# Three small changes of order in a hybrid attention block: where gate weights are prepared, where powers are taken, which weights are loaded first

## The chip, the cores and the metric

The kernel runs on one core of a Trainium2 chip, as one launch. The metric is device time in microseconds (us): the median of several runs of the kernel on the chip. Besides the runs there is one execution with the hardware profiler on. The core's engines are named as in the profile: TensorE is PE (with PEld for its weight loads), VectorE is DVE, ScalarE is ACT, GpSimd is POOL, SyncE is SP, and SPq is SP's queue, which issues nearly all transfers (DMA) of this kernel in one order.

## What is computed

A decoder layer of one sequence of 1024 tokens with 1024 features, in float32:

```
h    = rmsnorm(x)
proj = h @ w_in        # sliding-window q, k, v | query latents (384) | key/value latents (256)
                       # | rope key (32) | gate_a (1024) | gate_b (1024)
A    = sliding-window attention (8 heads, 2 key/value heads, window 128, a learned sink per head)
B    = latent attention: q = rmsnorm(q_lat) @ w_uq, k and v = rmsnorm(kv_lat) @ w_ukv, causal, 8 heads
y    = sigmoid(gate_a) * (A @ w_o_swa) + sigmoid(gate_b) * (B @ w_o_mla)
x    = x + y @ w_out
x    = x + (silu(h2 @ w_gate) * (h2 @ w_up)) @ w_down,   h2 = rmsnorm(x)
out  = rmsnorm(x)
```

## The kernel before

**Products.** Every float32 operand is split into a rounded high part and the rest, `hi` on ACT (line 159, a cast) and `lo` on DVE (line 162, a subtraction), and a product is three matmuls (lines 168 to 170). So each weight tile passes DMA, ACT and DVE before PE can use it. The large products are cut once into 2 x 2 blocks and done with seven block products in place of eight, named 1, 6, 2, 7, 5, 4, 3 in the order that they are taken. Sums of weight blocks that this needs are made on POOL (`mix`, `lower`). Products 1, 2, 5 and 3 add up in one PSUM bank (`fa`), products 6, 7 and 4 in another (`fb`). Between two of a bank's products its content is read out: after product 6 DVE adds `fb` and a saved tile into `pu` (`pu<-fb`), and only then may product 7 start to overwrite or add to `fb`.

**The gates.** The class `Seven` does the products for the 2048 gate columns, in eight groups j of seven products. `prep` splits the weights of one product (`wl`), `prep_to(n)` prepares up to the n-th product, `product` issues the next product's twelve matmuls on PE, and `copy_out` reads its bank. In `product` (line 685) the weights are prepared two products ahead, since `n_ahead` is 3. `gate_step` (line 746) runs one product with its read-out and then stores results that are ready.

**The stages.** The order of the first stage is written out by hand, as a string of two-letter steps (`ROWS`), and holds for all five engines. Its last rows begin the gates: `gp` is `prep_to`, `gx` is `product`, `ge` is `copy_out`; `gp5` stands behind `gx3 ge2 rr`. `rr` is a rotation of the rope key on POOL (`kr`, line 1051), and right behind the rows `kr` is stored. Then a loop of 15 iterations does the sliding-window attention, with three gate products in each as work for PE. One iteration has: transposes of the last block's probabilities (`pT<-per`, line 874), transposes of the queries, normalization of the present block's probabilities on POOL (`den` and `pe`, lines 844 to 847), the move of `pe` to `per` by DMA on SP's queue, the product with the values (`o`), and the next block's scores (`sc`), their maxima (line 816), shifts (`nm`, `es`) and exponentials (line 840).

The same loop also finishes the statistics of the latents: PE sums squares (line 765) into a spare piece of PSUM, `lat_stats` (line 1132) scales them on DVE into `rlat`, and, when both halves of the sequence are there, takes the power -1/2 of 8 columns on POOL (line 1137). That call stands ahead of the iteration's normalization, in iterations 2 (key/value latents) and 4 (query latents). `lat_tail` holds what follows at the end of an iteration: `lat_diag` in iteration 2 builds diagonals from the result on POOL (`dg`, line 1144), and `lat_norm` uses them on PE in iterations 3 and 5. The query part of `rlat` is first read in the latent attention.

**Behind the loop** five latent tiles (`ct`, line 1205) come back from DRAM, the two of keys and values first, then the three of queries; the weights for queries, keys and values (`uq`, `ukv`, lines 259 and 279) are loaded, split (`wuq`, `wv`) and used, `k<-ct,wv` for keys and `q<-ct,wuq` for queries, among the last four gate products. In the loop PE, SP and POOL keep the order of the program and a scheduler places ACT and DVE; behind the loop the scheduler, which works by its own estimate of times, places all of them.

Of the kernel before, what the change touches and what calls it, by code (L numbers as in the profile page):

```python
# [12 lines left out]
ALU = mybir.AluOpType  # L13
# [7 lines left out]
NB = S // P  # L21
# [66 lines left out]
def hybrid_block_kernel(  # L88
# [27 lines left out]
    nc = tc.nc  # L116
# [23 lines left out]
    def U(name, dt=F32, shape=(P, 1024)):  # L140
        return pool.tile(list(shape), dt, tag="u", name=uid(name))
# [7 lines left out]
    def P1(name, shape=(P, 512), dt=F32):  # L149
        return ps1.tile(list(shape), dt, tag="ps", name=uid(name))  # L150

    def PX(name, shape=(P, 512), dt=F32):
        return psum["x"].tile(list(shape), dt, tag="ps", name=uid(name))
# [3 lines left out]
    def split(hi, lo, src, eng=None):  # L157

        i = nc.scalar.copy(hi, src)  # L159
        if held[0]:  # L160
            tc.keep_in_program_order(i)
        (eng or nc.vector).tensor_tensor(lo, src, hi.bitcast(F32), op=ALU.subtract)  # L162

    def mm3(ps, pairs, first=True, last=True, go_on=False):

        n = len(pairs)
        for i, ((ah, al), (bh, bl)) in enumerate(pairs):
            nc.tensor.matmul(ps, ah, bh, start=first and i == 0, stop=False, skip_group_check=go_on)  # L168
            nc.tensor.matmul(ps, ah, bl, start=False, stop=False, skip_group_check=go_on)  # L169
            nc.tensor.matmul(ps, al, bh, start=False, stop=last and i == n - 1, skip_group_check=go_on)  # L170
# [10 lines left out]
    def half(s):  # L181
        return slice(512 * s, 512 * s + 512)
# [11 lines left out]
    rlat = const.tile([P, 2 * NB], F32, name="rlat")  # L194
    neg_half_w = const.tile([P, 2 * NB], F32, name="neg_half_w")
# [24 lines left out]
    st = Stream()  # L220
# [373 lines left out]
    class Seven:  # L594
# [87 lines left out]
            self.copy_out(*step)  # L682
            return step

        def product(self):
            j, q, m = self.seq[self.n_run]
            self.prep_to(self.n_run + self.n_ahead)
            self.n_run += 1
            if m == self.ms[0]:
                for what, *args in self.at.get((j, q), ()):  # L690
                    {"load": self.load_part, "mix": self.mix, "scale": self.scale_part}[what](*args)
            t = self.left.pop((j, q, m))
            if q in (1, 5):
                self.acc[("A", j, m)] = P1("fa")
            if q == 6:
                self.acc[("B", j, m)] = PX("fb")
            ps = self.acc[("A" if q in (1, 2, 5, 3) else "B", j, m)]
            rh, rl = hq[B_OF[q]]
            mm3(ps, [((t[:, 0, k], t[:, 1, k]), (rh[:, k], rl[:, k])) for k in range(4)], first=q in (1, 6, 5),
                go_on=q in (2, 7, 4, 3))  # L700
            return j, q, m
# [44 lines left out]
    def gate_step():  # L746
        late = gate_stores[:]
        gate_stores.clear()
        gates.run()
        for d, t in late:  # L750
            nc.sync.dma_start(d, t)

    gates = Seven(NK, "g", load_gate, gate_done, 3, (1, 6), 5, scale=scale_gate, scale_at=[(2, 0, 0, 2), (2, 0, 2, 2), (7, 1, 0, 2), (7, 1, 2, 2)], piece=2, vec=(2, 5))
# [347 lines left out]
    def small_tables():  # L1101
# [7 lines left out]
             "sl": load_set, "ss": set_sub, "sh": set_hi, "so": set_lo, "sf": set_four, "ph": phase, "tb": small_tables,  # L1109
             "ns": lambda: nc.vector.tensor_scalar(nsink, nsink, -1.0, None, op0=ALU.mult),  # L1110
             "gl": gates.load_part, "gs": gates.scale_part, "gm": gates.mix, "gp": gates.prep_to, "wq": sw_q, "wt": sw_qT,
             "gy": lambda j: gates.lower(j, "g"), "gx": lambda n: gates.product(),
             "ge": lambda n: gates.copy_out(*gates.seq[n - 1]), "wu": sw_q_hi, "wv": sw_q_lo,
             "wr": lambda it: sw_products(it, range(2)), "wm": lambda it: (sw_max(it, range(2)), sw_shift(it)),
             "we": sw_exp, "no": lambda it: sw[it].pop("norm")(), "mv": lambda it: nc.sync.dma_start(*sw[it].pop("move")),
# [11 lines left out]
    def lat_first():  # L1127
        ps = P1("st", (P, 4))
        sums(ps, 1, 0)
        lat_stats(ps, 1, 0)  # L1130

    def lat_stats(ps, grp, sh):
        c = slice(NB * grp + 4 * sh, NB * grp + 4 * sh + 4)
        nc.vector.tensor_scalar(rlat[:, c], ps[:, 0:4], -1.0 / (QL, KVL)[grp], EPS, op0=ALU.mult, op1=ALU.add)
        if sh:
            c = slice(NB * grp, NB * grp + NB)
            nc.gpsimd.tensor_tensor(rlat[:, c], rlat[:, c], neg_half_w[:, c], op=ALU.pow)

    def lat_diag():
        kvn["ones"] = U("ones", F32, (P, P))  # L1140
        nc.vector.memset(kvn["ones"], 1.0)
        kvn["dg"] = U("dg", F32, (P, NB, P))
        for b in range(NB):
            nc.gpsimd.tensor_scalar(kvn["dg"][:, b], ident, rlat[:, NB + b:NB + b + 1], 0.0, op0=ALU.mult, op1=ALU.add)

    def lat_norm(sh):
        ps = P1("rb", (P, 4, P))
        for b in range(4):
            nc.tensor.matmul(ps[:, b], kvn["ones"], kvn["dg"][:, 4 * sh + b], start=True, stop=True)
        for c in (3, 4):  # L1150
            y = klr[c][:, half(sh)]
            nc.vector.scalar_tensor_tensor(y, y, latg[:, c:c + 1], ps.rearrange("p b c -> p (b c)"), op0=ALU.mult,
                                           op1=ALU.mult)

    def kv_split(sh):
        for c in (3, 4):
            t = kvn[(c, sh)] = U("cs", F32R, (P, 2, 512))
            split(t[:, 0], t[:, 1], klr[c][:, half(sh)])

    def kv_store(sh):  # L1160
        for c in (3, 4):
            nc.sync.dma_start(ct_d[c][:, sh], kvn.pop((c, sh)).bitcast(F32))

    lat_tail = {1: lat_first, 2: lat_diag, 3: lambda: lat_norm(0), 4: lambda: kv_split(0),
                5: lambda: (kv_store(0), lat_norm(1)), 6: lambda: kv_split(1), 7: lambda: kv_store(1)}
    pool_order = tc.manual_schedule(engines={engines.Pool})
    pool_order.__enter__()
    for it in range(1, N_SW):
        if it + 2 < N_SW:
            sw_q(it + 2)  # L1170
        gate_step()
        sw_pT(it - 1)
        if it + 1 < N_SW:
            sw_qT_all(it + 1)
        if it in stats_at:
            lat_stats(spare[0], *stats_at[it])
        sw[it].pop("norm")()
        gate_step()
        nc.sync.dma_start(*sw[it].pop("move"))
        sw_pv(it - 1)  # L1180
        if it + 1 < N_SW:
            sw_scores(it + 1)
        gate_step()
        if it in lat_tail:
            lat_tail[it]()
# [16 lines left out]
    def load_ct(c):  # L1202
        t = V("ct", F32R, (P, 2, S))
        for sh in range(2):
            nc.sync.dma_start(t[:, :, half(sh)].bitcast(F32), ct_d[c][:, sh])
        lat_t.append((t[:, 0], t[:, 1]))
# [3 lines left out]
    for c in range(3, 5):  # L1210
        load_ct(c)
    gate_step()
    for c in range(3):
        load_ct(c)
    gate_step()
    st.load_to(st.index[("ukv", 1)])
    st.conv_to(st.index[("uq", 0)])
    gate_step()
    gate_step()
# [293 lines left out]
    for t in range(NT):  # L1513
        h, n = divmod(t, NB)
# [16 lines left out]
        if t in fill:  # L1531
            dc, sh, c0 = fill[t]
# [452 lines left out]
    while ffn.n_run < len(ffn.seq):  # L1985
        j, q, m = ffn.run()
# [211 lines left out]
```

## Time and profile before

| what | value |
|---|---|
| median of 3 runs | 1330.21 us (1328.77 to 1330.64) |
| the profiled execution: its time, its span | 1328.35 us, 1326.6 us |
| PE busy, share of the span | 1305.6 us, 98% |
| DVE, ACT, POOL busy | 928.5, 647.1, 587.7 us |
| gates' first products, sliding-window loop, weights and latents behind it | from about 136, 145 to 324, 320 to 345 us of the span |
| moved by DMA | 254.22 MB, mean 192 GB/s |

All times in rows are microseconds from the start of the span. A row of the timeline has its start, its length, the engine, the line, the operation, what is written and what is read (tile names without their numbers), and in brackets how long the engine stood idle before it and what ended that. A row of the waits has the waiting engine and line, what it waited for, and the total, the count and the longest wait in us. Matmuls are pipelined, so that a row's length is more than the distance from one start to the next; distances between starts are what counts for PE.

### The profile page before, as it was taken

The page shows a single profiled execution, that of the slowest core. Times are in us where ns is not written, and L with a number is a line of the kernel's source. Part 1 is how long each engine was busy: PE and PEld are TensorE (multiplying, and loading weights), DVE is VectorE, ACT ScalarE, POOL GpSimd, SP SyncE. Part 2 cuts the span into 40 slices and gives each one's busy share as a digit, 9 for nine tenths or more (in the row PEclk, how much of TensorE's full clock was granted, in tenths as well). Part 3 has the DMA queues.
Part 4 walks back from the last instruction along what each step waited for, and adds up shares of the span by engine and source line. Part 5 has one row for each costly group of instructions (what it writes and reads, how often), then busy time and mean ns, then how long its engine had stood idle before and what let it go on. Part 6 is the DMA issues. An engine that isn't in the chain of part 4 may idle for free.

```text
span 1326.6 us, 18712 instructions
## 1 busy us (share of the span) xinstructions
PE 1305.6 (98%) x6368; PEld 1093.4 (82%) x6368; DVE 928.5 (70%) x1451; ACT 647.1 (49%) x1285; POOL 587.7 (44%) x628
## 2 busy tenths in 40 slices
PE   9999899999999999999999999999999999999997
PEld 7987788888788889888888888888888888888886
DVE  7996678786577777887879756656676554663853
ACT  7586457666366666754455332323222223644451
POOL 3354566644225445412232465677676631022521
PEclk9999999999999999999999999999999999999999
DMA  9937327445688477798531334655444435995503
GB/s 355 331 123 203 135 97 257 160 169 191 220 272 200 101 223 159 246 342 193 186 126 51 111 127 167 223 209 210 183 172 151 154 112 197 372 395 210 175 24 135
DMA packets 94751, 254.22 MB, mean 192 GB/s; under 512 B 10560, under 2 KB 16320, under 8 KB 93504
## 3 DMA queue, kind: packets, MB, share of 16 engines
q1 hardware_dynamic: 89792, 242.35, 52.4%
q0 software_dynamic: 3424, 8.39, 3.6%
q10 hardware_dynamic: 1440, 2.27, 0.5%
q8 instruction: 51, 0.84, 0.3%
q14 instruction: 44, 0.36, 0.1%
HBM read 166.60 MB, written 82.18 MB: 188 GB/s over the span
## 4 chain that ended last, share of the span: by engine, by line
PE 65%; DVE 1%; issue 1%; ACT 1%; POOL 0%; POOLq 0%; ACTq 0%; DVEq 0%
PE fa L169 6%; PE fa L170 6%; PE fa L168 6%; PE fd L168 5%; PE fd L170 5%; PE fd L169 5%; PE fb L169 5%; PE fb L170 5%; PE fb L168 5%; PE xo L170 2%; PE xo L169 2%; PE xo L168 2%; PE pTb L1361 2%; PE oB L170 1%; PE oB L169 1%; PE oB L168 1%
## 5 line engine op out<-in xcount | busy, mean ns | idle before, releaser
L162 DVE TENSOR_TENSOR wl<-wr,wl 128x512 fp32r<-128x512 f32 x150 | 146.2, 998 | 70.7 <-ACT wl L159 70.1
L162 DVE TENSOR_TENSOR lrv<-lr,lrv 128x1024 fp32r<-128x1024 f32 x77 | 105.3, 1400 | 48.6 <-ACT lrv L159 43.6
L159 ACT CAST lrv<-lr 128x1024 fp32r<-128x1024 f32 x77 | 80.1, 1052 | 90.4 <-PE fd L170 53.9
L169 PE MATMUL fd<-lrv 128*128 128x512 f32 x308 | 119.8, 389 | 0.0
L168 PE MATMUL fd<-lrv 128*128 128x512 f32 x308 | 119.8, 389 | 0.0
L170 PE MATMUL fd<-lrv 128*128 128x512 f32 x308 | 119.8, 389 | 0.0
L173 POOL TENSOR_TENSOR wr<-wr,sm 128x512 f32<-128x512 f32 (+1 forms) x42 | 49.7, 1194 | 131.0 <-DVE wl L162 114.0
L159 ACT CAST wl<-wr 128x512 fp32r<-128x512 f32 x150 | 86.5, 620 | 3.3 <-DVE t3l L173 2.8
L162 DVE TENSOR_TENSOR wl<-sm,wl 128x512 fp32r<-128x512 f32 x60 | 51.3, 878 | 42.6 <-ACT wl L159 42.4
L1346 POOL TENSOR_TENSOR denb<-denb,neg_one 128x1 f32<-128x1 f32 x64 | 40.0, 625 | 87.9 <-ACT p L1345 63.3
L170 PEld LDWEIGHTS fd<-lrv 128*128 128x128 f32 x308 | 57.8, 188 | 12.1
L169 PEld LDWEIGHTS fd<-lrv 128*128 128x128 f32 x308 | 57.8, 188 | 12.0
L168 PEld LDWEIGHTS fd<-lrv 128*128 128x128 f32 x308 | 57.8, 188 | 11.9
L1345 ACT ACTIVATE p<-scb,nmb 128x384 f32<-128x384 f32 (+3 forms) x64 | 47.7, 745 | 32.5 <-DVE nmb L1344 21.8
L1344 DVE CUSTOM_DVE_ANT_0 scb<-scb,mask,rlat 128x384 f32<-128x384 f32 (+3 forms) x64 | 52.1, 818 | 13.5 <-PE scb L1336 13.4
L176 POOL TENSOR_TENSOR sm<-wr,wr 128x256 f32<-128x256 f32 (+1 forms) x42 | 46.9, 1118 | 28.5 <-ACT wr L911 14.2
L1719 ACT ACTIVATE act<-sm 128x512 f32<-128x512 f32 x11 | 7.0, 632 | 102.2 <-DVE sm L176 102.2
L168 PE MATMUL fb<-t3h,wl 128*128 128x512 f32 x132 | 52.2, 396 | 3.9 <-DVE pu L176 3.9
L162 DVE TENSOR_TENSOR ptl<-pTb,pth 128x512 fp32r<-128x512 f32 (+2 forms) x96 | 49.9, 549 | 7.2 <-ACT pth L159 6.7
L168 PE MATMUL fa<-hh,wl 128*128 128x512 f32 x132 | 52.5, 398 | 0.6 <-DVE klr L176 0.6
L159 ACT CAST pth<-pTb 128x512 fp32r<-128x512 f32 (+2 forms) x96 | 43.3, 480 | 18.6 <-PE pTb L1361 18.1
L173 POOL TENSOR_TENSOR wr<-wr 128x256 f32<-128x256 f32 (+1 forms) x42 | 52.2, 1244 | 0.0
(357 smaller groups left out, 4159.1 us busy)
## 6 DMA issues: line engine op xcount, KB each, us to landing
lr<-la_d SPq DMA_DIRECT2D x77, 256.0 KB, 5.1
wr<-in_w_gate_dram SPq DMA_DIRECT2D x22, 512.0 KB, 4.1
wr<-in_w_up_dram SPq DMA_DIRECT2D x22, 512.0 KB, 5.0
la_d<-sd SPq DMA_DIRECT2D x22, 512.0 KB, 5.1
wd<-in_w_down_dram SPq DMA_DIRECT2D x22, 512.0 KB, 6.6
rb_d<-wd SPq DMA_DIRECT2D x22, 512.0 KB, 2.6
lr<-rb_d SPq DMA_DIRECT2D x44, 256.0 KB, 5.3
lr<-in_w_down_dram SPq DMA_DIRECT2D x33, 256.0 KB, 5.1
```

The lines of the kernel that those rows point to most:

```text
L159: i = nc.scalar.copy(hi, src)
L162: (eng or nc.vector).tensor_tensor(lo, src, hi.bitcast(F32), op=ALU.subtract)
L168: nc.tensor.matmul(ps, ah, bh, start=first and i == 0, stop=False, skip_group_check=go_on)
L169: nc.tensor.matmul(ps, ah, bl, start=False, stop=False, skip_group_check=go_on)
L170: nc.tensor.matmul(ps, al, bh, start=False, stop=last and i == n - 1, skip_group_check=go_on)
L173: eng.tensor_tensor(out, a, b, op=ALU.subtract)
L176: eng.tensor_tensor(out, a, b, op=ALU.add)
L1344: nc.vector.tensor_tensor_reduce(s_, s_, m_, rlat[:, n:n + 1], -NEG, op0=ALU.add, op1=ALU.min, accum_out=nm)
L1345: nc.scalar.activation(p_, s_, AF.Exp, scale=-1.0, bias=nm, accum_out=den)
L1346: nc.gpsimd.tensor_tensor(den, den, neg_one[:, 0:1], op=ALU.pow)
L1361: nc.tensor.transpose(pp[:, i], p[:, blk(k0 + i)], ident)
L1719: nc.scalar.activation(dst, src, AF.Silu)
```

## The change

It has three parts. First, `product` gets an argument, and the hand-written steps `gx1`, `gx2`, `gx3` no longer prepare weights ahead; only the `gp` steps of the rows do. For `gx1` and `gx2` nothing changes, since `gp3` and `gp4` stand next to or ahead of them; the weights of the fifth product (product 5) are now prepared by `gp5`, behind `ge2` and `rr`, not ahead of `gx3`'s matmuls. Second, the powers become a function of their own, `lat_root`, called at the ends of iterations 2 and 4, behind the normalization. Third, the loads of the weights `uq` (second unit) and `ukv` stand ahead of the three query latents, not behind them and one gate product.

```diff
-        def product(self):
+        def product(self, ahead=True):
             j, q, m = self.seq[self.n_run]
-            self.prep_to(self.n_run + self.n_ahead)
+            if ahead:
+                self.prep_to(self.n_run + self.n_ahead)
...
-             "gx": lambda n: gates.product(),
+             "gx": lambda n: gates.product(False),
...
     def lat_stats(ps, grp, sh):
         c = slice(NB * grp + 4 * sh, NB * grp + 4 * sh + 4)
         nc.vector.tensor_scalar(rlat[:, c], ps[:, 0:4], -1.0 / (QL, KVL)[grp], EPS, op0=ALU.mult, op1=ALU.add)
-        if sh:
-            c = slice(NB * grp, NB * grp + NB)
-            nc.gpsimd.tensor_tensor(rlat[:, c], rlat[:, c], neg_half_w[:, c], op=ALU.pow)
+
+    def lat_root(grp):
+        c = slice(NB * grp, NB * grp + NB)
+        nc.gpsimd.tensor_tensor(rlat[:, c], rlat[:, c], neg_half_w[:, c], op=ALU.pow)
...
-    lat_tail = {1: lat_first, 2: lat_diag, 3: lambda: lat_norm(0), 4: lambda: kv_split(0),
+    lat_tail = {1: lat_first, 2: lambda: (lat_root(1), lat_diag()), 3: lambda: lat_norm(0), 4: lambda: (lat_root(0), kv_split(0)),
...
     gate_step()
+    st.load_to(st.index[("ukv", 1)])
     for c in range(3):
         load_ct(c)
     gate_step()
-    st.load_to(st.index[("ukv", 1)])
```

The change also moves instructions that the diff does not name. On DVE, at the end of the hand-written rows, before (`es` ends the shifts of a block, `wl<-sm` is product 5's weights, `pu<-fb` the read of bank `fb` behind product 6, `sm<-fb` that behind product 7):

```order
L827 TENSOR_TENSOR es_1565<-nm_1563,nsink 128x4
L162 TENSOR_TENSOR wl_1575<-sm_1430,wl_1575 128x512
L176 TENSOR_TENSOR pu_1542<-fb_1545,pu_1542 128x512
L176 TENSOR_TENSOR sm_1430<-fb_1545,pu_1542 128x512
L162 TENSOR_TENSOR wl_1606<-wr_1044,wl_1606 128x512
L162 TENSOR_TENSOR ptl_1628<-pT_1629,pth_1627 128x512
```

And the same place on DVE now:

```order
L828 TENSOR_TENSOR es_1565<-nm_1563,nsink 128x4
L176 TENSOR_TENSOR pu_1542<-fb_1545,pu_1542 128x512
L162 TENSOR_TENSOR wl_1593<-sm_1430,wl_1593 128x512
L162 TENSOR_TENSOR wl_1606<-wr_1044,wl_1606 128x512
L176 TENSOR_TENSOR sm_1430<-fb_1545,pu_1542 128x512
L162 TENSOR_TENSOR ptl_1628<-pT_1629,pth_1627 128x512
```

The read of `fb` has changed places with the split of product 5's weights, and the split for product 4 (`wl_1606`) with the second read.

On POOL in iteration 2 of the loop, before (`rlat` is the power, `den` and `pe` the normalization, `wr<-wr,sm` a sum of gate weights, `dg` the diagonals):

```order
L1137 TENSOR_TENSOR rlat<-rlat,neg_half_w 128x8
L844 TENSOR_TENSOR den_1703<-den_1703,es_1701 128x4
L845 TENSOR_TENSOR den_1703<-den_1703,neg_one 128x4
L847 TENSOR_SCALAR pe_1704<-pe_1704,den_1703 128x256 x4
L173 TENSOR_TENSOR wr_1403<-wr_1403,sm_1654 128x2x128 x2
L1144 TENSOR_SCALAR dg_1870<-ident_r,rlat 128x128 x8
```

And the same place on POOL now:

```order
L845 TENSOR_TENSOR den_1703<-den_1703,es_1701 128x4
L846 TENSOR_TENSOR den_1703<-den_1703,neg_one 128x4
L848 TENSOR_SCALAR pe_1704<-pe_1704,den_1703 128x256 x4
L173 TENSOR_TENSOR wr_1403<-wr_1403,sm_1654 128x2x128 x2
L1139 TENSOR_TENSOR rlat<-rlat,neg_half_w 128x8
L1146 TENSOR_SCALAR dg_1870<-ident_r,rlat 128x128 x8
```

The power has moved behind the normalization and behind the sum of weights. In iteration 1, just ahead of this, the four operations on `kr` now stand between the four of `pe`, not behind them.

On SP's queue behind the loop, before (`ct_3674`, `ct_3677` and `ct_3680` are the query latents, `krt` the rope key, `oa` a result of the loop):

```order
L1205 DMA ct_3674<-ct_d 128x2x512 x2
L896 DMA oa_d<-oa_3303 128x1024
L1209 DMA krt_3647<-kr_d 128x256
L1205 DMA ct_3677<-ct_d 128x2x512 x2
L1205 DMA ct_3680<-ct_d 128x2x512 x2
L259 DMA wr_3700<-in_w_uq_dram 128x768
L279 DMA wr_3702<-in_w_ukv_dram 128x1024
L279 DMA wr_3704<-in_w_ukv_dram 128x1024
```

And the same place on SP's queue now:

```order
L1207 DMA ct_3680<-ct_d 128x2x512 x2
L897 DMA oa_d<-oa_3303 128x1024
L1211 DMA krt_3647<-kr_d 128x256
L259 DMA wr_3674<-in_w_uq_dram 128x768
L279 DMA wr_3676<-in_w_ukv_dram 128x1024
L279 DMA wr_3678<-in_w_ukv_dram 128x1024
L1207 DMA ct_3683<-ct_d 128x2x512 x2
L1207 DMA ct_3686<-ct_d 128x2x512 x2
```

The three weight loads have moved ahead of two of the query latents, four transfers; the first query latent stays in front. With this the scheduler places PE's work there in another order: before, eleven matmuls `q<-ct,wuq` stood between the transposes of `krt` and gate product 4, and the rest behind the key products; now gate product 4 comes first, then the transposes, gate product 3, the key products `k<-ct,wv`, and all of `q<-ct,wuq` behind them. DVE splits the weights of gate products 4 and 3 ahead of product 5's read-out, no longer behind it, and ACT and DVE split all of `ukv` ahead of the transposed rope key.

More of the change, by code (lines that the diff above doesn't have):

```diff
@@ L1111, in hybrid_block_kernel @@
              "gl": gates.load_part, "gs": gates.scale_part, "gm": gates.mix, "gp": gates.prep_to, "wq": sw_q, "wt": sw_qT,
-             "gy": lambda j: gates.lower(j, "g"), "gx": lambda n: gates.product(),
+             "gy": lambda j: gates.lower(j, "g"), "gx": lambda n: gates.product(False),
              "ge": lambda n: gates.copy_out(*gates.seq[n - 1]), "wu": sw_q_hi, "wv": sw_q_lo,
```

## The prediction

> **What bounds the kernel now.** I read the busy time of stretches first, to see which engine fills the span and where it does not (columns: length, then busy us and instructions of PE, of its weight loads, DVE, ACT and POOL; PE's granted clock, DMA share, GB/s).
>
> ```profile
> 118.00:160.00 42.00, 37.45 (x173) 29.83 (x173) 24.58 (x59) 21.46 (x59) 25.22 (x35) 0.96 0.47 162
> 160.00:206.00 46.00, 44.52 (x248) 37.24 (x247) 36.00 (x81) 29.85 (x78) 28.58 (x44) 1.00 0.39 135
> 334.00:372.00 38.00, 36.60 (x166) 29.49 (x165) 23.41 (x38) 15.58 (x29) 10.12 (x8) 1.00 0.61 216
> sum 1326.00, PE 1305.60 PEld 1093.35 DVE 928.47 ACT 647.09 POOL 587.67; mean PE 163.20 PEld 136.67 DVE 116.06 ACT 80.89 POOL 73.46
> ```
>
> TensorE (PE) is busy 1305.60 of 1326 us; the change removes no matmul, so it can gain only PE's waits and its slow clock. The three stretches it touches hold 4.55, 1.48 and 1.40 us of PE idle time, and the first alone has a granted clock under 1. The waits of PE over the whole span name what ends them (total, times, longest, in us):
>
> ```profile
> PE fb L168 <- DVE pu L176: 3.9, 2, 3.4
> PE pT L874 <- DMA per<-pe: 1.4, 2, 1.2
> PE k L168 <- ACT wv L159: 0.8, 1, 0.8
> PE k L170 <- DVE wv L162: 0.6, 1, 0.6
> ```
>
> They answer one to one to the three edits. Each is now read from the timeline.
>
> **Part 1, gate weights only where the order has them.** First PE at the largest wait, then the vector engine (DVE) and the scalar engine (ACT) at the same time; then twelve matmuls without a wait, for their spacing.
>
> ```profile
> 141.97 0.39 PE L170 MATMUL fa<-hh,wl 128*128 128x512 f32 x1
> 145.77 0.50 PE L168 MATMUL fb<-t3h,wl 128*128 128x512 f32 x1 [3.42 <-DVE pu L176]
> ...
> 146.81 0.51 PE L169 MATMUL fb<-t3l,wl 128*128 128x512 f32 x1
> ...
> 150.10 0.57 PE L874 MATMUL pT<-ident_r,per 128*128 128x128 f32 x4
> ...
> 161.34 0.80 PE L874 MATMUL pT<-ident_r,per 128*128 128x128 f32 x8
> ...
> 170.50 0.39 PE L168 MATMUL fa<-hh,wl 128*128 128x512 f32 x1
> ...
> 173.00 0.39 PE L170 MATMUL fa<-hh,wl 128*128 128x512 f32 x1
> 174.63 0.84 PE L874 MATMUL pT<-ident_r,per 128*128 128x128 f32 x8 [1.25 <-DMA per<-pe]
> ...
> 199.04 0.39 PE L170 MATMUL fb<-t2h,wl 128*128 128x512 f32 x1
> 199.61 0.85 PE L874 MATMUL pT<-ident_r,per 128*128 128x128 f32 x8 [0.19 <-DMA per<-pe]
> ```
>
> ```profile
> 140.46 1.31 DVE L825 SCALAR_TENSOR_TENSOR nm<-mx,nsink 128x4 f32<-128x4 f32 x1
> 141.80 0.17 DVE L827 TENSOR_TENSOR es<-nm,nsink 128x4 f32<-128x4 f32 x1
> 144.43 0.69 DVE L162 TENSOR_TENSOR wl<-sm,wl 128x512 fp32r<-128x512 f32 x1 [2.46 <-ACT wl L159]
> 145.03 0.68 DVE L176 TENSOR_TENSOR pu<-fb,pu 128x512 f32<-128x512 f32 x1
> ```
>
> ```profile
> 143.77 0.63 ACT L159 CAST wl<-sm 128x512 fp32r<-128x512 f32 x1
> ```
>
> From 170.50 to 173.00 lie 11 spacings, so a 128x512 matmul normally starts 0.227 us after the last. The step gx3 prepares, ahead of its own product, the weights of the fifth; this puts the DVE half of that split (wl<-sm) in front of pu<-fb, the read that clears the PSUM bank fb. wl<-sm needs ACT's cast, and that starts at 143.77 only, behind the exponentials in ACT's order. So DVE sits idle for 2.46 us with work that could run, and PE, whose next product goes into fb, waits for it. The price: 145.77 - 141.97 - 0.227 = 3.57 us, and after the gap PE runs at half rate: 8 spacings from 146.81 to 150.10 take 3.29 us where 8 x 0.227 = 1.82 would do, another 1.47. Together 5.04.
>
> In the new order pu<-fb follows es. It can start at 141.97 at the latest, ends at 142.65, and PE began 0.06 us after its end (145.03 + 0.68 = 145.71, then 145.77), so 142.71. PE would be free at 142.20: 0.51 us of the wait stays, set by the score maxima ahead on DVE. I charge that as a plain wait without the slow clock, because the 1.25 us wait at 174.63 is followed by no slow matmuls (0.84 us for eight transposes, like the 0.85 at 199.61). Gain 5.04 - 0.51 = 4.53; without the clock's part it would be 3.06. Nothing else of the step moves PE: the weights wl<-sm are now wanted at 142.71 + 12 x 0.227 plus six transposes, about 145.9, and are done at 145.12 as before, since ACT is not touched. That leaves 0.8 us of cover; were it gone, the split would cost what it is late by, at most the 0.7 us of its own length.
>
> [...]
>
> **Part 2, the powers behind the normalization.** The GpSimd engine (POOL) and its feeders at the second wait, and the first work that needs the power's result:
>
> ```profile
> 165.13 2.15 POOL L1137 TENSOR_TENSOR rlat<-rlat,neg_half_w 128x8 f32<-128x8 f32 x1 [9.09 <-DVE rlat L1134]
> 167.25 0.20 POOL L844 TENSOR_TENSOR den<-den,es 128x4 f32<-128x4 f32 x1
> ...
> 168.63 1.84 POOL L847 TENSOR_SCALAR pe<-pe,den 128x256 f32<-128x256 f32 x4
> 170.44 1.44 POOL L173 TENSOR_TENSOR wr<-wr,sm 128x256 f32<-128x256 f32 x2
> 171.85 3.68 POOL L1144 TENSOR_SCALAR dg<-ident_r,rlat 128x128 f32<-128x128 f32 x8
> ```
>
> ```profile
> 160.04 0.21 ACT L840 ACTIVATION_READ_ACCUMULATOR pe<-sc,nm 128x1 f32 x1
> ```
>
> The exponentials are done at 160.25, but POOL stands idle for 9.09 us at the power, which waits for sums that PE and DVE make later. The normalization (167.25 to 170.47, 3.22 us) then runs late, and the store, move and transposes hang on it: 1.63 - 0.227 = 1.40 us at 174.63, and 0.57 - 0.227 = 0.34 at 199.61 behind the second power. In the new order it runs from 160.25 to 163.5; the move takes until about 167.6 (as today 170.47 to 174.63), PE wants it at 173.23: 5.6 us to spare. The power goes behind the two wr subtractions, at about 165, and dg ends about 165.1 + 2.15 + 3.68 = 170.9, before today's 175.5, so the matmuls on dg lose nothing. Moved past it are the den, pe and wr steps alone; none waits longer. The other power's result is first used by the latent attention, far later. Gain 1.74.
>
> POOL's order also puts the four small kr operations between the pe steps of iteration 1, whose move the SyncE queue (SPq) issues behind a store of kr:
>
> ```profile
> 150.94 0.50 SPq L1179 DMA_DIRECT2D per<-pe  x1
> ```
>
> The work up to the later of the two is the same, so the move is issued no later than now. At the 4.1 us from pe's end to the transposes it has landed by 155.1; the transposes that want it run at 161.34 now and 4.53 sooner then, at 156.8: 1.7 us of cover, and beyond it every us costs one.
>
> **Part 3, key and value weights ahead of three latents.** PE at the third wait, then ACT, DVE and SPq:
>
> ```profile
> 337.21 0.47 PE L168 MATMUL q<-ct,wuq 128*128 128x512 f32 x1
> ...
> 344.36 0.39 PE L170 MATMUL k<-ct,wv 128*128 128x512 f32 x1
> 345.55 0.50 PE L168 MATMUL k<-ct,wv 128*128 128x512 f32 x1 [0.80 <-ACT wv L159]
> ...
> 347.21 0.40 PE L168 MATMUL k<-ct,wv 128*128 128x512 f32 x1
> ```
>
> ```profile
> 340.79 1.14 ACT L159 CAST wv<-wr 128x512 fp32r<-128x512 f32 x2 [9.07 <-DMA wr<-in_w_ukv_dram]
> ...
> 343.53 0.62 ACT L159 CAST wv<-wr 128x512 fp32r<-128x512 f32 x1 [0.51 <-DMA wr<-in_w_ukv_dram]
> ```
>
> ```profile
> 341.45 1.29 DVE L162 TENSOR_TENSOR wv<-wr,wv 128x512 fp32r<-128x512 f32 x2 [4.07 <-ACT wv L159]
> ```
>
> ```profile
> 326.99 2.57 SPq L1205 DMA_DIRECT2D ct<-ct_d  x4
> 329.62 1.11 SPq L259 DMA_DIRECT2D wr<-in_w_uq_dram  x1
> 330.77 1.53 SPq L279 DMA_DIRECT2D wr<-in_w_ukv_dram  x2
> ```
>
> Four spacings from 344.36 to 347.21 take 2.85 us instead of 0.91: 1.94 lost while the last weights arrive. Now the three weight loads stand ahead of the last four latent loads, so the key and value weights are issued at about 328.1, not 330.77. By that alone they land 2.6 us sooner, at 338.2 and 340.9; with two MB no longer ahead of them, sooner still. PE's order is changed too: the eleven query matmuls that filled PE before the last gate products now come behind the key products, so the key products start at 344.36 - 2 x 0.227 - 11 x 0.227 = 341.4, and want the second half at 342.1. From the cast's start at 340.79 to the end of the DVE half (341.45 + 1.29) it takes 1.95 us, so even the late bound is ready near 342.9 and leaves 0.4 us of wait at the third matmul. Gain between 1.5 and 1.94; I take 1.94, nearer to the case with the latents out of the way.
>
> What is late next are those latents: 1.4 MB of weights (384 + 2 x 512 KB) now precede the last one, at the stretch's mean of 216 GB/s 6.5 us later. Today its first use starts at 337.21, with no wait that counts in the list above; so it lands by 343.7 at the worst, and is first used at 341.4 + 18 x 0.227 = 345.5. Covered by 1.8 us.
>
> **Sum.** 4.53 + 1.74 + 1.94 = 8.2 us. The profiled execution took 1328.35 us (span 1326.6), which gives 1320.1 against itself; it lies 1.86 below the median of the runs, 1330.21, and from that the same sum gives 1322.0, which I forecast. The engines behind these places follow PE (DVE is busy 36.00 of 46.00 us in the second), so I expect the shift to be carried to the end.
>
> **Rivals.**
> (a) The loads keep their own pace. PE comes to the keys 4.53 + 1.74 = 6.3 us sooner, but the SyncE queue does not: the last latent lands at 343.7 and is wanted at 345.5 - 6.3 = 339.2; 4.5 us go back, 3.7 stay: 1326.5. Against it: the issues around 327 wait on PE's and DVE's results, so they should move along. 0.15.
> (b) The slow clock is not in the other runs of before: 6.7, so 1323.5. For it: one profile shows it, once. 0.15.
> (c) Part 1 does not do what it says, the bank's wait being for something else named wrongly: gain 3.7, 1326.5. Against it: pu's end and PE's start fit to 0.06 us. 0.06.
> (d) Slower: the latents become the bound. If the 1.4 MB and the four latents (3.5 MB) come at the 135 GB/s of the second stretch, from 327 on, the last lands at 353; wanted at 339.2 that is a wait of 13.8 us, with 1.5 of slow clock after it, against 8.2 gained: 7.1 slower, 1337.3. It turns slower once the last latent lands after about 346. For it: one queue carries it all; against: the stretch itself averages 216 GB/s with a DMA share of 0.61. 0.03.
> The forecast itself gets 0.58; 0.03 is for a loss elsewhere that leaves no difference.
>
> **Range and chances.** A measurement can tell about 0.2%, 2.7 us, from no change. The forecast with (b), and the runs' own spread of 1.9 us, span 1319.5 to 1324.5; to hold 8 in 10 the range must take in (a) and (c) as well: 1319.5 to 1326.8. Faster 0.91 (the forecast, a, b, c, less a little of each that falls short), same 0.06, slower 0.03.
>
> **What would show it.** Right: no wait of over 1 us on fb<-t3h, and a clock of 1.00 from 118 to 160; no wait of pT on per<-pe at the third and fifth iteration; no wait of k on wv. Wrong: a wait of q on ct near 340 (a, d), a slow stretch near 145 though the gap is short, wl<-sm ending a PE wait, or the same waits turning up later under other names with PE's idle sum still near 21 us.

## The result, and the profile after

| | before | changed |
|---|---|---|
| median beside each other, first group | 1328.74 us (6 runs) | 1320.84 us (1319.17 to 1322.66, 6 runs) |
| ratio, 95% interval | | 0.9941 (0.9928 to 0.9955) |
| second group of runs | 1327.67 us (11 runs) | 1320.72 us (1319.01 to 1323.12, 6 runs) |
| ratio, 95% interval | | 0.9945 (0.9929 to 0.9961) |
| the profiled execution: time, span | 1328.35, 1326.6 us | 1322.27, 1320.5 us |
| PE busy | 1305.6 us | 1303.4 us |

The change makes the kernel 7 to 8 us faster; forecast were 8.2. The spans of the profiled executions differ by 6.1 us only, and 1.2 of these were there before the first edited place (row 141.97 of before is row 140.79 below, behind the same instructions). So the profile holds the three gains and something that goes the other way.

The stretches of the prediction come first, then one more that the prediction did not read (length, busy us of PE, its weight loads, DVE, ACT, POOL, then the granted clock):

```profile
118.00:160.00 42.00, 40.07 (x198) 32.22 (x199) 25.71 (x63) 24.59 (x67) 28.01 (x39) 1.00 0.49 175
160.00:206.00 46.00, 45.95 (x250) 38.67 (x249) 37.72 (x94) 31.19 (x85) 28.77 (x43) 1.00 0.43 158
334.00:372.00 38.00, 38.00 (x170) 31.54 (x169) 20.60 (x35) 13.95 (x26) 10.05 (x8) 1.00 0.64 209
400.00:440.00 40.00, 36.91 (x228) 32.27 (x227) 30.35 (x59) 24.50 (x56) 19.45 (x26) 0.96 0.51 126
```

PE's idle time went from 4.55 to 1.93 us, from 1.48 to 0.05 and from 1.40 to nothing, and the clock of the first stretch is back at 1.00. But from 400 to 440 PE is idle for 3.09 us, at a clock of 0.96, where before it was idle for 1.93 us at a clock of 1.00:

```profile
400.00:440.00 40.00, 38.07 (x237) 32.88 (x238) 31.29 (x63) 26.76 (x61) 20.80 (x28) 1.00 0.64 153
```

The waits of PE in the changed kernel name both what is left and what is new:

```profile
PE pTb L1363 <- DVE ob L1397: 2.1, 2, 1.9
PE o L887 <- DVE ptl L162: 0.8, 1, 0.8
PE fb L168 <- DVE pu L176: 0.7, 2, 0.5
```

The three waits that the change was aimed at are gone (that on `fb` is down from 3.42 to 0.27 us at this place; the one of 0.5 was there before too); `o` on `ptl` and a `pTb` of 1.9 us are new. The timeline of the changed kernel at the first edited place, with the engines that PE waits for:

```profile
140.70 0.69 DVE L176 TENSOR_TENSOR pu<-fb,pu 128x512 f32<-128x512 f32 x1
140.79 0.39 PE L170 MATMUL fa<-hh,wl 128*128 128x512 f32 x1
141.44 0.50 PE L168 MATMUL fb<-t3h,wl 128*128 128x512 f32 x1 [0.27 <-DVE pu L176]
...
144.30 0.46 PE L875 MATMUL pT<-ident_r,per 128*128 128x128 f32 x4
...
144.64 1.44 POOL L1052 TENSOR_TENSOR kr<-kr,lg 128x256 f32<-128x256 f32 x2
...
146.11 0.62 ACT L159 CAST wl<-wr 128x512 fp32r<-128x512 f32 x1 [2.41 <-POOL kr L1052]
146.76 0.75 DVE L162 TENSOR_TENSOR wl<-wr,wl 128x512 fp32r<-128x512 f32 x1 [2.82 <-ACT wl L159]
147.56 0.39 PE L886 MATMUL o<-pth,vv 128*128 128x512 f32 x1
148.04 0.67 DVE L162 TENSOR_TENSOR ptl<-pT,pth 128x512 fp32r<-128x512 f32 x1
148.77 0.49 PE L887 MATMUL o<-ptl,vv 128*128 128x512 f32 x1 [0.82 <-DVE ptl L162]
...
150.55 0.40 PE L168 MATMUL fb<-t4h,wl 128*128 128x512 f32 x1
```

`pu<-fb` now starts at 140.70, right behind the shifts, and PE gets bank `fb` 0.42 us late (141.44 - 140.79 - 0.227). From 140.79 to the transposes it takes 3.51 us, where before took 8.13 (141.97 to 150.10). Behind that the new wait shows: ACT sits idle for 2.41 us until the rope rotation on POOL ends (144.64 + 1.44 = 146.08, and the cast starts at 146.11), DVE sits idle for that cast, so `ptl` is late, and PE with it.

Before, the first matmul of the fifth `fb` product came 4.81 us behind the transposes (150.10), and now it comes 6.25 us behind them (144.30 to 150.55):

```profile
154.91 0.40 PE L168 MATMUL fb<-t4h,wl 128*128 128x512 f32 x1
```

So 1.44 of the 4.62 us go back here. At the second and third place nothing waits any more; the same instructions as before, now:

```profile
168.59 0.40 PE L170 MATMUL fa<-hh,wl 128*128 128x512 f32 x1
168.82 0.80 PE L875 MATMUL pT<-ident_r,per 128*128 128x128 f32 x8
...
337.51 0.39 PE L170 MATMUL k<-ct,wv 128*128 128x512 f32 x1
337.73 0.39 PE L168 MATMUL q<-ct,wuq 128*128 128x512 f32 x1
```

The gain is then partly given back in the latent attention, some 80 us behind the last edit. Before, there:

```profile
420.75 1.38 SPq L1414 DMA_DIRECT2D sg<-gate_d  x1
...
427.66 1.06 ACT L1417 ACTIVATE sg<-sg 128x1024 f32<-128x1024 f32 x1 [0.95 <-DMA sg<-gate_d]
...
429.39 0.40 PE L1336 MATMUL scb<-kT,qT 96*128 96x512 f32 x1
430.74 1.06 PE L1361 MATMUL pTb<-ident_r,p 128*128 128x128 f32 x6 [0.95 <-DVE ob L1395]
...
434.34 0.39 PE L1336 MATMUL scb<-kT,qT 96*128 96x512 f32 x1
```

And the same instructions in the changed kernel:

```profile
412.39 1.05 SPq L1416 DMA_DIRECT2D sg<-gate_d  x1
...
420.20 1.06 ACT L1419 ACTIVATE sg<-sg 128x1024 f32<-128x1024 f32 x1 [1.88 <-DMA sg<-gate_d]
421.01 0.40 PE L1338 MATMUL scb<-kT,qT 96*128 96x512 f32 x1
423.29 1.07 PE L1363 MATMUL pTb<-ident_r,p 128*128 128x128 f32 x6 [1.88 <-DVE ob L1397]
...
424.87 0.63 PE L1338 MATMUL scb<-kT,qT 96*128 96x512 f32 x1
...
428.19 0.40 PE L1338 MATMUL scb<-kT,qT 96*128 96x512 f32 x1
```

Subtract row from row: PE comes 8.38 us sooner at 421.01, but only 7.45 sooner at `pTb` and 6.15 sooner at 428.19. The first 0.93 us is a longer wait for `sg<-gate_d`, a load of gates. The load was issued 8.36 us sooner (420.75, now 412.39), as much as PE came sooner, but from its issue to the tanh that waits for it passed 7.81 us, where before 6.91 passed. ACT keeps its tanh on that tile in the order of the program, ahead of the next exponentials and of the copy `otb`, which `ob` on DVE and with it `pTb` need. The other 1.3 us is a slow stretch behind that wait (the granted clock from 424.39 to 427.81 is 0.50).

### The profile page after: what moved, and what is told of

The parts are those of the page before. It is cut to its first block, busy times and chain, and to the rows that moved or that the text cites. A ratio compares the mean times of both kernels' runs of the same rounds, so it can differ in the third digit from the quotient of the medians.

```text
span 1320.5 us, 18722 instructions
## 1 busy us (share of the span) xinstructions
PE 1303.4 (99%) x6368; PEld 1092.2 (83%) x6368; DVE 928.1 (70%) x1451; ACT 647.1 (49%) x1285; POOL 589.0 (45%) x628
## 4 chain that ended last, share of the span: by engine, by line
PE 65%; issue 1%; POOL 1%; DVE 1%; ACT 0%; POOLq 0%; ACTq 0%
PE fa L170 6%; PE fa L169 6%; PE fa L168 6%; PE fd L168 5%; PE fd L169 5%; PE fd L170 5%; PE fb L169 5%; PE fb L170 5%; PE fb L168 5%; PE xo L170 2%; PE xo L168 2%; PE xo L169 2%; PE pTb L1363 1%; PE oB L170 1%; PE oB L168 1%
## 5 line engine op out<-in xcount | busy, mean ns | idle before, releaser
L162 DVE TENSOR_TENSOR wl<-wr,wl 128x512 fp32r<-128x512 f32 x150 | 143.5, 980 | 73.2 <-ACT wl L159 72.7
L168 PE MATMUL fa<-hh,wl 128*128 128x512 f32 x132 | 52.6, 398 | 0.3 <-DVE klr L176 0.3
L170 PE MATMUL fa<-hh,wl 128*128 128x512 f32 x132 | 51.9, 393 | 0.4 <-DVE wl L173 0.4
```

## The experiments

Ten runs; each time stands beside runs of the kernel before on the same chip (medians of 1327.94 us for the first four, 1327.67 for the next four, 1327.53 for the last two).

**Part 1 alone.** The edit is the one of `product` and `gx`, made to the kernel before.

> Part 1 alone, on the kernel before. Theory (a place moved): taking product 5's weights behind the rope rotation also gives the split weights of product 4 another place in memory, one that the rope operations on GpSimd still read; ScalarE's cast for product 4 waits for them, and PE pays at the products with the values. Then the stretch from the last matmul of the third gate product to the first of the fifth bank-fb product shrinks from 12.94 us to about 9.8, there is a wait of about 0.8 us of o on ptl, and the run is 3.2 us faster (1.7 if the slow clock behind the old gap is absent from the runs of before). The waits of pT on per and of k on wv stay as they were, within 0.5 us. Rival (the forecast as it stood): the stretch shrinks to 8.4 us, no wait at o, 4.5 us faster.

1324.74 us, ratio 0.9985 (0.9975 to 0.9996): 3.2 us by the medians and 2.0 by the ratio, not 4.5. The stretch to the fifth `fb` product takes 9.74 us, with a wait of 0.80 us of `o` on `ptl`, as the theory had it. One thing neither side had: the wait behind the power, which this kernel still has, grew from 1.25 to 1.56 us, and a slow stretch followed (a granted clock of 0.50 for 6.83 us). PE and POOL of this run, and its granted clock:

```profile
161.76 2.15 POOL L1138 TENSOR_TENSOR rlat<-rlat,neg_half_w 128x8 f32<-128x8 f32 x1 [8.22 <-DVE rlat L1135]
...
168.55 0.39 PE L170 MATMUL fa<-hh,wl 128*128 128x512 f32 x1
170.49 0.85 PE L875 MATMUL pT<-ident_r,per 128*128 128x128 f32 x8 [1.56 <-DMA per<-pe]
```

```profile
171.68:178.51 6.83, 6.83 (x21) 5.57 (x21) 3.22 (x7) 3.40 (x8) 4.03 (x8) 0.50 0.33 126
```

128x512 matmuls start 0.43 us apart there, 0.23 ahead of it. At a clock of 0.50 for 6.83 us PE loses about 3.4, my estimate from the two numbers: in this profile part 1 has given all its gain back by 179.

**Part 2 alone.** `lat_root` behind the normalization, in the kernel before.

> Part 2 alone, on the kernel before. Theory: the two waits of pT on per (1.25 and 0.19 us) go, the wait on bank fb of 3.4 us stays with its slow clock, and the run is 1.7 us faster. Rival (the wait is an effect of PE being early, taken up by the next thing late): the gain is given back at the diagonals or at the keys, where the wait of 0.8 us grows to 2.5, and the run is within 0.3 us of before.

1326.05 us, ratio 0.9984 (0.9975 to 0.9993): 1.9 us by the medians. Both waits of `pT` on `per` are gone, the wait on `fb` (3.4 us) stays with its half clock (0.50 from 145.29 to 148.70), and at the keys PE waits 0.6 us, no more than before. The theory holds at these places. Further on, though, the wait of `pTb` that the changed kernel has is here as well, with a clock of 0.50 from 428.59 to 432.00 behind it, so that this profile gives a part of the gain back too:

```profile
427.65 1.06 PE L1362 MATMUL pTb<-ident_r,p 128*128 128x128 f32 x6 [1.57 <-DVE ob L1396]
```

**Part 3 alone.** The loads of `uq` and `ukv` ahead of the query latents, in the kernel before.

> Part 3 alone, on the kernel before. Theory: the waits of k on wv (0.8 and 0.6 us) go, none of q on a latent comes, and the run is 1.9 to 2.1 us faster. Rival (a give-back by loads): PE comes 2 us sooner to the attention's first gate product while its gate load keeps its time; the wait of pTb on ob near 430 grows from 0.95 to over 1.5 us with a slow stretch behind it, and the run is within 0.5 us of before.

1326.23 us, ratio 0.9992 (0.9983 to 1.0001): 1.7 us by the medians, though the interval does not exclude that there is no gain. The waits of `k` on `wv` are gone, `q` waits for no latent, and `pTb` at 426.35 waits for nothing, so the give-back of the changed kernel is not made by this part alone.

**Product 5's weights one step earlier.** In the changed kernel:

```diff
-         ro23 gx2 wm1 mv0 gy0 we1 gx3 ge2 rr gp5 ge3 ro15 ro12
+         ro23 gx2 wm1 mv0 gy0 we1 gx3 ge2 gp5 rr ge3 ro15 ro12
```

> The changed kernel with gp5 one step earlier, ahead of the rope rotation and still behind ge2. Theory (a place moved): memory places are again as before, ScalarE's cast for product 4 waits for no rope operation, the wait of o on ptl (0.82 us) and the late query split behind it go, the stretch to the first matmul of the fifth bank-fb product falls from 9.76 to 8.2 to 8.7 us, and the run is 1.0 to 1.6 us faster than the changed kernel, so 8.9 to 9.5 faster than before. Rival (PE is simply too early for the engines behind the transposes, whatever the place): the wait at o stays within 0.3 us of 0.82 and the time is that of the changed kernel, 7.9 below before.

1321.13 us, ratio 0.9955 (0.9942 to 0.9967): no faster than the changed kernel. My expectation was wrong, and the timeline tells why:

```profile
146.35 1.43 POOL L1052 TENSOR_TENSOR kr<-kr,lg 128x256 f32<-128x256 f32 x2
...
147.81 0.58 ACT L159 CAST pth<-pT 128x512 fp32r<-128x512 f32 x1 [3.67 <-POOL kr L1052]
...
148.44 0.50 PE L886 MATMUL o<-pth,vv 128*128 128x512 f32 x1 [0.80 <-ACT pth L159]
```

The cast of `wl` no longer waits for the rotation, but now the cast of `pth` does, to the same 0.03 us behind its end (146.35 + 1.43 = 147.78). Neither cast reads or writes `kr` or its table `lg`. The waits that the compiled programs carry say what happens; ACT's two casts before and in this variant, and then in the changed kernel:

```
L159 CAST wl_1606<-wr_1044 128x512
L159 CAST pth_1627<-pT_1629 128x512 [waits DMAHW0_49,DMAHW6_49,PE_49,Pool_49]

L159 CAST wl_1606<-wr_1044 128x512 [waits DMAHW0_49,Pool_49]
L159 CAST pth_1627<-pT_1629 128x512 [waits DMAHW1_49,PE_49]
```

Tiles take their memory in turn from a pool, in the order in which the program asks. Taking product 5's weights behind `rr` moved all of them on by one place, so that the memory of `lg` went to `wl` and no longer to `pth`. Whoever gets it must wait until the rotation has read the table. The addresses in the compiled programs say the same: `lg` and `pth_1627` share one before and in this variant, `lg` and `wl_1606` in the changed kernel. Before the change the wait was there too, on `pth`, and cost nothing, since the rotation ended at 148.60 and PE's transposes came at 150.10 only.

**The changed kernel again**, as it is, for what varies from one execution to the next, above all the wait of 1.88 us of `pTb` in the latent attention and the slow stretch behind it.

> The changed kernel as it is, once more, beside the others of this group. [...] About 7.9 us faster than before. Rival: the late pTb and its slow stretch belong to the change and come again, of the same 1.9 us within 0.2.

The times are in the table above. `pTb` waited 1.96 us again, with a clock of 0.50 behind it from 425.34 to 428.75: the rival was right, in both profiles of the changed kernel the gate load comes this late (7.88 us from its issue to the tanh, against 7.81).

**Parts 1 and 2 together**, without part 3.

> Parts 1 and 2 together, without part 3. Theory (the parts lean on each other): part 1 alone brought PE to the second iteration's transposes 4 us sooner while GpSimd's normalization stood behind the power, so 1.56 us of wait and 6.8 us of half clock ate its gain; with part 2 in, that wait and that slow stretch are gone, and the run is 5.5 to 6.5 us faster than before, more than the 3.2 and 1.9 of the two alone. Rival (they simply add): 5.1 us or less, with a slow stretch near 170.

1322.00 us, ratio 0.9961 (0.9945 to 0.9977): 5.7 us by the medians, where the two alone make 5.1 in sum. The medians can't tell that apart, but the profile can: the transposes that waited 1.56 us with part 1 alone start at 169.00, 0.24 us behind the matmul ahead of them, with no slow stretch. In these profiles part 1 needs part 2. `pTb` waits here as well, but less:

```profile
424.04 1.07 PE L1363 MATMUL pTb<-ident_r,p 128*128 128x128 f32 x6 [0.52 <-DVE ob L1397]
```

**The rope rotation earlier.** In the changed kernel:

```diff
-         ro23 gx2 wm1 mv0 gy0 we1 gx3 ge2 rr gp5 ge3 ro15 ro12
+         ro23 gx2 rr wm1 mv0 gy0 we1 gx3 ge2 gp5 ge3 ro15 ro12
```

> The changed kernel with the rope rotation rr moved ahead, behind gx2, and gp5 right behind ge2. GpSimd, idle for 2.2 us before the normalization, does the rotation there. Theory (memory held by the rotation is what ScalarE waits for, under whichever name): ScalarE's casts for product 4 and for pth wait for no kr, the wait of PE at o (0.82 us in the changed kernel, 0.80 under another name with gp5 moved alone) falls below 0.3 us, and the stretch to the fifth bank-fb product falls from 9.76 to 8.2 to 8.6 us; the run is 1 to 1.6 us faster than the changed kernel. Rival (PE too early for DVE and ScalarE whatever GpSimd does): the wait at o stays between 0.6 and 1.0.

1319.88 us, ratio 0.9936 (0.9921 to 0.9950); the changed kernel beside it took 1320.72. That is 0.8 us, less than the 1 to 1.6 expected, and the intervals of the two overlap. The timeline settles it better than the time:

```profile
141.66 1.44 POOL L1052 TENSOR_TENSOR kr<-kr,lg 128x256 f32<-128x256 f32 x2
141.84 0.39 PE L170 MATMUL fa<-hh,wl 128*128 128x512 f32 x1
...
144.59 0.65 ACT L159 CAST wl<-wr 128x512 fp32r<-128x512 f32 x1
...
148.81 0.39 PE L887 MATMUL o<-ptl,vv 128*128 128x512 f32 x1
...
149.99 0.40 PE L168 MATMUL fb<-t4h,wl 128*128 128x512 f32 x1
```

The rotation is done by 143.1, the cast follows ACT's other work at once, `o` waits for nothing, and the stretch to the fifth `fb` product falls from 9.76 to 8.15 us (141.84 to 149.99). So 1.6 us of part 1's gain had gone into the wait for the memory of `lg`. PE was not too early for the others.

**The rotation and the gate loads earlier.** As the last, and in the latent attention the load stands ahead of the mixing product:

```diff
+         if t in g_at:
+             load_sig(g_at[t])
          if t in fill:
              dc, sh, c0 = fill[t]
              mix_a(dc, sh, c0, 2, P1("oA") if c0 == 0 else None)
...
-         if t in g_at:
-             load_sig(g_at[t])
```

> As the kernel with the rotation moved, and in the latent attention each gate load is issued ahead of the mixing product of its step, not behind the store that waits for that product. Theory (the load keeps its pace while PE comes sooner): the second gate load is issued about 16 us sooner, ScalarE's tanh waits for no load, the wait of pTb on ob (1.9 us in the changed kernel) and the slow stretch behind it are gone, and the run is 1 to 3 us faster than the kernel with the rotation moved alone, near 1317 to 1319. Rival (DVE's ob is late for another reason): the wait stays over 1 us.

1317.64 us (1316.69 to 1318.69), ratio 0.9922 (0.9907 to 0.9936), the fastest of all. The load is issued at 398.58 (in the changed kernel at 412.39, behind a store that waits for a mixing product; 13.3 us sooner than with the rotation moved alone, where about 16 were expected), the tanh waits for nothing, and `pTb` of PE for nothing either:

```profile
398.58 0.34 SPq L1416 DMA_DIRECT2D sg<-gate_d  x1
...
415.50 1.07 ACT L1419 ACTIVATE sg<-sg 128x1024 f32<-128x1024 f32 x1
...
419.53 0.82 PE L1363 MATMUL pTb<-ident_r,p 128*128 128x128 f32 x6
```

**The gate loads alone**, in the changed kernel.

> The changed kernel with the gate loads of the latent attention issued ahead of the mixing product, and nothing else. Theory (a load that keeps its pace took back what the change won): the wait of pTb on ob (1.88 and 1.96 us in two profiles of the changed kernel) and the slow stretch behind it go, 2 to 2.5 us at that place; the wait of o on ptl of 0.8 us stays; the run is 1.5 to 2.5 us faster than the changed kernel, near 1318.5. Rival (the 2.2 us less of the kernel with both edits came from the order of PE, which this edit also moves): the wait goes but the run is within 0.5 us of the changed kernel.

1318.69 us, ratio 0.9937 (0.9923 to 0.9951): about 2 us faster than the changed kernel by the medians, 0.5 to 1.1 us by the ratios, whose intervals overlap. The wait of `o` (0.8 us) is still there, that of `pTb` is 0.3 us at the longest, and the mean granted clock of the profiled execution is 0.998, where the changed kernel has 0.997. The late load, then, is what this wait came from; the time that it is worth is known less well.

**A squaring step later**, on top of both, to see what the last 0.42 us on bank `fb` wait for.

```diff
-         ... rh23 rl23 wr1 es23 ge1
-         ro23 gx2 rr wm1 mv0 gy0 we1 gx3 ge2 gp5 ge3 ro15 ro12
+         ... rh23 rl23 wr1 ge1
+         ro23 gx2 rr wm1 mv0 gy0 we1 gx3 ge2 gp5 es23 ge3 ro15 ro12
```

> The kernel with the rotation and the gate loads moved, and a squaring step (es23, on ScalarE and GpSimd) moved behind gp5. In every profile DVE's nm took 1.3 us where it takes 0.16 elsewhere, and it began and ended with GpSimd's addition sq (138.99 to 140.27). Theory (the two hold each other up): without sq at its side nm takes 0.2 us, pu starts 1.1 us sooner, and the last 0.42 us of the wait on bank fb go; the run gains about 0.4 us, less than a measurement can tell. Rival (nm waits for its inputs): nm still takes 1.3 us and the wait stays.

1319.29 us, ratio 0.9940 (0.9927 to 0.9953): `nm` does what the theory says, and the run is no faster than the kernel with both edits. With the squares at its side (the kernel with both edits), DVE's `nm` began and ended with POOL's `sq`:

```profile
138.99 1.30 DVE L826 SCALAR_TENSOR_TENSOR nm<-mx,nsink 128x4 f32<-128x4 f32 x1
138.99 1.28 POOL L176 TENSOR_TENSOR sq<-sq,sqt 128x512 f32<-128x512 f32 x1
```

Without them:

```profile
139.12 0.16 DVE L826 SCALAR_TENSOR_TENSOR nm<-mx,nsink 128x4 f32<-128x4 f32 x1
...
146.81 1.26 POOL L176 TENSOR_TENSOR sq<-sq,sqt 128x512 f32<-128x512 f32 x1
148.10 0.69 DVE L162 TENSOR_TENSOR ptl<-pT,pth 128x512 fp32r<-128x512 f32 x1 [2.42 <-POOL sq L176]
148.85 0.49 PE L887 MATMUL o<-ptl,vv 128*128 128x512 f32 x1 [1.83 <-DVE ptl L162]
150.78 0.63 PE L168 MATMUL fb<-t4h,wl 128*128 128x512 f32 x1
```

`nm` takes 0.16 us, and the last wait on `fb` at this place is gone. But `ptl` now has the memory that `sq`'s operand held, and waits for it (146.81 + 1.26 = 148.07, then 148.10): 1.83 us at `o`, and a clock of 0.50 behind it from 150.42 to 153.83. It is the same mechanism a third time, under a third name.

## Why the prediction was right, and where it was not

**The number.** 8.2 us were forecast, 7.9 and 7.0 measured by the medians. Two losses that the sum did not have, 1.4 and 2.2 us in the profile, should have left less, so it is in part luck that the measured gain lies this near to the forecast. The profile makes 4.9 us without the difference at its start (3.2 + 1.7 + 2.2 - 2.2); that start varies from profile to profile (the last matmul of the third gate product lies between 140.42 and 141.97 in the twelve of this case, and that of before is the latest). How the other runs come to more than 4.9 us stays open; both profiled executions of the changed kernel (1322.27 us, span 1320.5; span 1320.6) lie above its medians. The prediction had named one sign of being wrong that came true in part: waits that turn up later under other names. PE's idle time in the whole span (span less busy) is 17.1 us, where before it was 21.0.

**Part 1, 4.53 forecast, 3.18 came.** The mechanism was right, and the price at its place nearly exact: to the transposes 4.62 us were won, the wait of 3.57 us and its slow clock are gone, and 0.42 us are left where I had 0.51. The step that failed is "Nothing else of the step moves PE". I followed the weights of product 5 alone. The edit also moved which tile gets the rotation's memory, and 1.44 of the 4.62 us went back at `o`. I had looked at the interleaved `kr` on POOL, and asked only who reads what it writes, not who waits for what it reads from.

**Part 2, 1.74 forecast, 1.73 came.** 1.40 us at 168.82, where the transposes follow at the normal spacing (0.23 us), and 0.33 at the second place (the shift to before there is 0.33 more than ahead of it). No work on `dg` is late. What the sum missed is in the other direction: with part 1 in, the wait would not have stayed at 1.25 us but grown to 1.56 with a slow stretch, so part 2 also protects part 1.

**Part 3, 1.94 forecast, about 2.2 came.** The shift against before is 6.14 us at the transposes of 199.61 (now 193.47) and 8.38 at 421.01; some 0.1 of the difference lies ahead of the keys. The keys and queries wait for nothing, and the latents are not late: rivals (a) and (d), at the place that they named, did not come.

**"I expect the shift to be carried to the end"** is the second step that failed. In the latent attention PE came 8.38 us sooner to the matmuls ahead of `pTb`, but the wait there grew by 0.93 us, and 1.3 us of half clock came with it. Rival (a) comes to mind, a load with a pace of its own, but that is not what happened: the load stands behind a store that waits for DVE's last work on a mixing product, and its issue moved along by 8.36 us. What changed is how long it took from there. The profiles with the load at its old place (issue, us from the issue to the start of the tanh, ACT's wait for the load):

| kernel | issue | to the tanh | wait |
|---|---|---|---|
| part 3 alone | 417.34 | 5.92 | none |
| part 1 alone | 419.40 | 6.00 | none |
| parts 1 and 2 | 414.51 | 6.44 | 0.52 |
| before | 420.75 | 6.91 | 0.95 |
| product 5's weights earlier | 414.36 | 7.28 | 1.35 |
| part 2 alone | 417.07 | 7.50 | 1.58 |
| the rotation earlier | 411.88 | 7.55 | 1.61 |
| changed | 412.39 | 7.81 | 1.88 |
| changed, again | 412.56 | 7.88 | 1.96 |

In each row with a wait, the time to the tanh less the wait is 5.9 us: ACT always wants the tile 5.9 us after its issue, and the wait is what the load takes longer. How much sooner PE comes does not decide that: with part 2 alone the load is issued 3.7 us sooner than before and takes 7.50 us, with parts 1 and 2 it is issued 6.2 us sooner and takes 6.44. Why it takes longer in one kernel than in another stays open. The row that gives the warning, a wait of 0.95 us of `pTb` behind a tanh that waits for a load, was in the trace of before: a wait of that size on a load means no cover at all.

**Rival (b)**, that the slow clock is not in other runs of before: against it, all three profiles that have the old gap of 3.4 us have a clock of 0.50 behind it (before from 146.94, part 2 alone from 145.29, part 3 alone from 145.18). **Rival (c)**, a misnamed wait, fell with part 1 alone: the wait on `fb` at this place shrank from 3.42 to 0.26 us.

## What to carry to other kernels

Where tiles take memory in turn from a pool, an edit that moves one allocation hands every later one another predecessor: compare the waits of the compiled instructions, not only their order, on all engines near the edit. When PE is made earlier, list every load that it already waits for further on, however briefly. Such a load has no cover, even where its issue moves along with PE: whatever it takes longer in the new kernel goes straight into the wait (here 0.90 us longer, and 0.93 us more of wait), unless it is issued further ahead. A wait removed upstream can make the next one worse (part 1 without part 2: 1.25 us became 1.56), so edits of this kind are costed in the order in which PE meets them.

## What the runs showed of the hardware

**The half clock came in stretches of one length.** Each slow stretch that was read ahead of PE's last matmul had a granted clock of 0.50 and lasted 3.41 us (3.42 in the changed kernel) or twice that (6.83 with part 1 alone). In one trace the starts of two of them lie a whole number of such lengths apart: with part 2 alone 145.29 and 428.59, 283.3 us, 83 x 3.413, and 3.413 us is the length of the stretch in the clock record of the traces of before and of the changed kernel. Waits of PE of 3.4, 1.96, 1.88, 1.83, 1.57 and 1.56 us were followed by one; one of 1.61 us (the rotation earlier, clock 1.00 around it), one of 1.35 (product 5's weights one step earlier) and those of 0.95 and 1.25 in before (clock 1.00 in both stretches) were not. And one of 0.80 with smaller ones beside it (again product 5's weights one step earlier, 0.50 from 150.77 to 154.18) was; the mean clock of 0.998 over that span of 1320.8 us leaves no room for a second stretch. So the length of the single wait does not decide it; what does is not settled.

**`nm` on DVE takes as long as `sq` on POOL beside it.** `nm`, an operation on 128x4 elements, took 1.30 us beside the POOL addition `sq` and 0.16 us without it; in the two rows of the last experiment they start together and end within 0.02 us of each other. Before (1.31 us beside 1.29) and in the changed kernel (1.30 beside 1.29) it was so too. `sq` itself took 1.28 us beside `nm` and 1.26 without, so of the two it is `nm` that is held up. Why is not shown.
